# Attention scores of both maps in one PSUM tile of five banks, with one maximum and one exponential per map

## The chip, the cores and the metric

The kernel runs on one core of a Trainium2 chip. A core has five engines, each with its own queue that runs in order: TensorE (PE) multiplies matrices and writes PSUM; VectorE (DVE), ScalarE (ACT) and GpSimd (POOL) work element by element; SyncE (SP) issues transfers. PSUM is 16 KB per partition, eight banks of 512 fp32 numbers. Engines wait for each other through semaphores that the program sets. The metric is the time in microseconds of one whole execution on the device.

## The reference, cut to what matters

The program is one step of a network with two layers, for a prompt of 256 tokens and a sample of 1024. The change lies in the differential attention of layer 0: per head two score maps, two softmaxes, and the difference of the two applied to the values. The sample sees 256 cached keys as well as its own 1024.

```python
def _diff_attn(q, k, v, lam):          # 8 heads (H_B), 2 maps, DH = 64
    ...
    def block(qi):                     # 128 queries
        s = jnp.einsum('bqhmd,bkhmd->bhmqk', qi.astype(F32), kf) * (DH ** -0.5)
        p = jax.nn.softmax(s, axis=-1)
        a = p[:, :, 0] - lam * p[:, :, 1]
        return jnp.einsum('bhqk,bkhe->bqhe', a, vf)
    ...
# sample: k = 256 cached keys and 1024 own ones; prompt: its own 256
```

## The kernel before, in words

The attention is `stage_b`. Its unit is a tile of 128 queries of one head. A head has ten: tiles 0 to 7 (`qt < 8`) are the sample's, with 1280 keys, and tiles 8 and 9 the prompt's, with 256. Eight heads follow each other, 80 tiles in all. The loop at the end of `stage_b` is written as a software pipeline, and the order in it is the order on the engines PE, DVE, ACT and POOL (`tc.manual_schedule`). In the round of tile t:

- PE: `scores(t)`, twelve matmuls (per map 1024 sequence keys in two halves of 512 and 256 cached keys, each once with the queries' high part `qh` and once with the low part `ql`); in tiles 8 and 9 a step of the next head's value projection (`PRE`); two transposes of the tile before last (`turn(p, 8)`); every second tile the value product of a pair (`values`, 30 matmuls, `pv`); steps of a projection that fills gaps (`FILL`, 24 matmuls a step, `acc`); eight transposes of the last tile (`turn(u, 0)`, `turn(u, 4)`).
- DVE: `maxima(t, 0)`, `maxima(t, 1)`, `ratio(t)`, `combine(t, 0)`, then the low parts `atl` of the transposes.
- ACT: `exps(t, 0)`, `exps(t, 1)`, then casts of weights (`whi`) and of transposes (`ath`), copies, and the scaling in `combine(t, 1)`, whose sum POOL makes.

The scores lie in three PSUM tiles: X0 and X1 (two banks each, 1024 sequence keys of map 0 and 1) and Y (one bank, the cached keys of both maps side by side; in tiles 8 and 9 the prompt's keys). Two more PSUM pools hold the transposes (`pt`, two buffers of one bank) and the products (`pa`, one bank). So a map has two maxima, joined by a minimum of their negatives (L1007), two exponentials, and two sums, joined in `ratio` (L1020). X0 and X1 also serve as PSUM for the value transposes `vt` of the next head (ten in tile 9, L948) and X1 for a small product `mp` (16 matmuls at the end of tile 9, read by DVE at L85; in the last head in tile 8).

A PSUM tile is the unit by which the framework keeps order: what writes or reads it waits for the other engines' earlier work on the same tile.

```python
seq(0)                                               # X0
for m in range(2):
    dot(t.Y[:, m], m, hd.kx[m][:, LS:] if t.qt < 8 else hd.kp[m])
seq(1)                                               # X1
```

Of the kernel before, what the change touches and what calls it, by code (L numbers as in the profile page):

```python
# [904 lines left out]
def stage_b(c, wp):  # L905
# [5 lines left out]
    with ExitStack() as es:  # L911
# [18 lines left out]
        def value_steps(h):  # L930
# [12 lines left out]
            for i in range(0, 10, n):  # L943
                w = min(n, 10 - i)
                p = (ps.tile([128, 8, 128], F32, name="vt", tag=f"X{i // 8}") if h else
# [32 lines left out]
        def scores(t):  # L978

            t.X, t.Y = [None] * 2, ps.tile([128, 2, 256], F32, name="Y")  # L980
            q, hd = t.q, t.hd
            t.mx = sm.tile([128, 2, 2], F32, name="mx")
            t.sums = sm.tile([128, 2, 2], F32, name="sums")
            t.e = [wk.tile([128, 1280], F32, name=f"e{m}", bufs=3 - m) for m in range(2)]

            def dot(out, m, keys):
# [3 lines left out]
            def seq(m):  # L990
                if t.qt < 8:
                    t.X[m] = ps.tile([128, 1024], F32, name=f"X{m}", tag=f"X{m}")
                    for k in (0, 512):
                        dot(t.X[m][:, k:k + 512], m, hd.kx[m][:, k:k + 512])
            seq(0)
            for m in range(2):
                dot(t.Y[:, m], m, hd.kx[m][:, LS:] if t.qt < 8 else hd.kp[m])
            seq(1)

        def maxima(t, m):  # L1000
            b = t.mx[:, 1, m:m + 1]
# [1005 lines left out]
```

## Time and profile before

| | |
|---|---|
| median of 3 runs | 2843.38 us (2842.13 to 2846.84) |
| the profiled execution | 2840.99 us, of it 2839.2 us span |
| PE, DVE, ACT, POOL busy in the span | 91%, 64%, 38%, 23% |
| `stage_b`, from the first score | 788 to about 1500 us |
| one head in it (heads 2 to 7) | about 88 us |

A row of a timeline gives start, length, engine, line and operation with output<-input, and in brackets how long the engine had stood idle and what ended it. A matmul's end is modelled: the next starts some 0.23 us after it (512 columns) although its row is 0.39 us long. Rows of equal instructions are merged (x10).

### The profile page before, as it was taken

The page shows a single profiled execution, that of the slowest core. Times are in us where ns is not written, and L with a number is a line of the kernel's source. Part 1 is how long each engine was busy: PE and PEld are TensorE (multiplying, and loading weights), DVE is VectorE, ACT ScalarE, POOL GpSimd, SP SyncE. Part 2 cuts the span into 40 slices and gives each one's busy share as a digit, 9 for nine tenths or more (in the row PEclk, how much of TensorE's full clock was granted, in tenths as well). Part 3 has the DMA queues.
Part 4 walks back from the last instruction along what each step waited for, and adds up shares of the span by engine and source line. Part 5 has one row for each costly group of instructions (what it writes and reads, how often), then busy time and mean ns, then how long its engine had stood idle before and what let it go on. Part 6 is the DMA issues. An engine that isn't in the chain of part 4 may idle for free.

```text
span 2839.2 us, 40047 instructions
## 1 busy us (share of the span) xinstructions
PE 2587.4 (91%) x14905; PEld 2254.6 (79%) x14905; DVE 1826.1 (64%) x3570; ACT 1072.1 (38%) x2136; POOL 660.4 (23%) x508
## 2 busy tenths in 40 slices
PE   8999889986689999999988789988999999999998
PEld 6777777765578888888876667767999989999786
DVE  6889999997367778777777962575234435654332
ACT  3342233211156667666663221463223333322311
POOL 0000000000023223232234443316223324432321
PEclk9999999987899999999999899998999999999999
DMA  5534566466722222122216772322322136654422
GB/s 221 179 113 116 168 205 199 160 200 164 186 73 81 86 81 80 54 90 86 75 58 192 240 246 84 108 86 80 109 78 74 61 98 225 202 169 152 148 79 93
DMA packets 232490, 368.76 MB, mean 130 GB/s; under 512 B 31044, under 2 KB 155494, under 8 KB 228710
## 3 DMA queue, kind: packets, MB, share of 16 engines
q1 hardware_dynamic: 200520, 315.03, 34.9%
q10 hardware_dynamic: 31632, 50.53, 6.0%
q8 instruction: 117, 1.92, 0.3%
q14 instruction: 77, 0.63, 0.1%
q0 software_dynamic: 144, 0.66, 0.1%
HBM read 248.82 MB, written 104.73 MB: 125 GB/s over the span
## 4 chain that ended last, share of the span: by engine, by line
PE 41%; DVE 14%; ACT 5%; DMA 4%; POOL 2%; issue 2%; SPq 0%; DVEq 0%; ACTq 0%; POOLq 0%
PE pf L47 6%; PE pf L46 6%; PE pf L48 6%; PE oa L48 3%; PE oa L47 3%; PE oa L46 3%; DVE mx L1003 2%; ACT e L1013 2%; DVE mrt L131 2%; DVE atl L1047 2%; PE acc L46 1%; PE acc L47 1%; PE acc L48 1%; DVE e L1031 1%; DMA owf<-w_out_o 1%
## 5 line engine op out<-in xcount | busy, mean ns | idle before, releaser
L48 PE MATMUL acc<-hhi,wlo 128*128 128x512 f32 (+1 forms) x1152 | 414.0, 361 | 32.2 <-DVE wlo L42 32.2
L46 PE MATMUL acc<-hhi,whi 128*128 128x512 f32 (+1 forms) x1152 | 417.8, 363 | 11.1 <-ACT O L1056 6.5
L47 PE MATMUL acc<-hlo,whi 128*128 128x512 f32 (+1 forms) x1152 | 414.3, 360 | 0.8 <-DVE hlo L218 0.2
L1034 POOL TENSOR_TENSOR e<-e,e 128x1024 f32<-128x1024 f32 x64 | 152.5, 2382 | 1104.1 <-DMA vh<-dVc 799.7
L48 PEld LDWEIGHTS acc<-hhi,wlo 128*128 128x128 f32 x1152 | 220.2, 191 | 70.0 <-DVE wlo L42 39.6
L48 PE MATMUL oa<-owh,oyl 128*128 128x512 f32 x640 | 254.3, 397 | 6.3 <-POOL oyl L42 6.3
L46 PEld LDWEIGHTS acc<-hhi,whi 128*128 128x128 f32 x1152 | 220.8, 192 | 46.5 <-ACT O L1056 11.0
L46 PE MATMUL oa<-owh,oyh 128*128 128x512 f32 x640 | 253.6, 396 | 2.3 <-ACT gt L1269 1.1
L47 PE MATMUL oa<-owl,oyh 128*128 128x512 f32 x640 | 252.9, 395 | 0.0
L47 PEld LDWEIGHTS acc<-hlo,whi 128*128 128x128 f32 x1152 | 220.6, 191 | 33.2 <-DVE hlo L218 3.4
L1013 ACT ACTIVATE e<-X,mx 128x1024 f32<-128x1024 f32 x128 | 142.8, 1116 | 120.7 <-DVE mx L1007 117.6
L42 POOL TENSOR_TENSOR wlo<-wf,whi 128x512 fp32r<-128x512 f32 x80 | 111.2, 1389 | 297.0 <-ACT whi L41 277.9
L41 ACT CAST whi<-wf 128x512 fp32r<-128x512 f32 x146 | 89.7, 620 | 211.1 <-DMA wf<-w_glu 43.7
L1003 DVE TENSOR_REDUCE mx<-X 128x1 f32<-128x1024 f32 x128 | 155.2, 1212 | 18.0 <-PE X L988 18.0
L42 DVE TENSOR_TENSOR wlo<-fold,whi 128x512 fp32r<-128x512 f32 x94 | 85.4, 922 | 108.0 <-ACT whi L41 107.0
L48 PEld LDWEIGHTS oa<-owh,oyl 128*128 128x128 f32 x640 | 120.8, 189 | 37.6 <-POOL oyl L42 9.9
L46 PEld LDWEIGHTS oa<-owh,oyh 128*128 128x128 f32 x640 | 120.7, 189 | 32.4 <-DVE t L1366 2.1
L1366 DVE TENSOR_TENSOR t<-oa,gate 128x512 f32<-128x512 f32 x60 | 41.3, 690 | 160.2 <-PE oa L48 157.2
L47 PEld LDWEIGHTS oa<-owl,oyh 128*128 128x128 f32 x640 | 120.7, 189 | 27.9
L1046 ACT CAST ath<-atp 128x512 fp32r<-128x512 f32 (+1 forms) x208 | 99.3, 513 | 103.2 <-PE atp L1043 101.8
L46 PE MATMUL pf<-heh,whi 128*128 128x322 f32 x400 | 126.0, 319 | 9.9 <-ACT heh L1527 8.2
L1047 DVE TENSOR_TENSOR atl<-atp,ath 128x512 fp32r<-128x512 f32 (+1 forms) x208 | 115.2, 579 | 18.5 <-ACT ath L1046 18.5
(450 smaller groups left out, 6969.9 us busy)
## 6 DMA issues: line engine op xcount, KB each, us to landing
wf<-w_in_e SPq DMA_DIRECT2D x96, 256.0 KB
raw<-w_fno SPq DMA_DIRECT2D x16, 1024.0 KB
mw<-w_mod SPq DMA_DIRECT2D x24, 512.0 KB
stg<-w_modT SPq DMA_DIRECT2D x24, 512.0 KB
u<-dU SPq DMA_DIRECT2D x16, 640.0 KB
dz<-z SPq DMA_DIRECT2D x8, 1280.0 KB
zc<-dz SPq DMA_DIRECT2D x16, 640.0 KB
qh<-dQh SPq DMA_DIRECT2D x160, 64.0 KB
```

Of the source, the lines that this page charges most:

```text
L41: nc.scalar.copy(hi, src)
L42: (le or nc.gpsimd).tensor_sub(lo, src, hi.bitcast(F32))
L46: nc.tensor.matmul(out, whi, xhi, start=start, stop=False)
L47: nc.tensor.matmul(out, whi, xlo, start=False, stop=False)
L48: nc.tensor.matmul(out, wlo, xhi, start=False, stop=stop)
L131: nc.vector.scalar_tensor_tensor(t, w, 0.5, s.cond[:, g], op0=OP.mult, op1=OP.mult, accum_out=acc[:, g:g + 1])
L1003: v.tensor_reduce(t.mx[:, 0, m:m + 1], t.X[m], axis=AX.X, op=OP.max, negate=True)
L1013: nc.scalar.activation(t.e[m][:, :LS], t.X[m], AF.Exp, bias=b, accum_out=t.sums[:, 0, m:m + 1])
L1034: nc.gpsimd.tensor_add(e[0][:, nk:], e[0][:, nk:], e[1][:, nk:])
L1046: nc.scalar.copy(hi, p[:, :w])
L1047: return lambda: v.tensor_sub(t.al[:, b:b + w, o], p[:, :w], hi.bitcast(F32))
L1366: nc.vector.tensor_mul(t, acc[j, m], gate(j // 8)[:, o])
```

## The change

One tile S of five banks, 2560 numbers per partition, takes the place of X0, Y and X1 for the whole stage. Map 0 has columns 0 to 1279 and map 1 columns 1280 to 2559, so that the third bank holds the end of map 0 and the start of map 1. The twelve matmuls stay, in the order map 0 first half, map 0 second half, map 1's first 256 keys, map 0's cached keys, then the rest of map 1. One maximum and one exponential over 1280 columns serve a map; the sum goes straight to where `ratio` reads it, and the minimum (L1007) and the addition (L1020) fall away. Tiles 8 and 9 use columns 1024 to 1535. `vt` takes columns 0 to 1023 and from 1536 on, `mp` columns 1536 to 1663.

```diff
+        S = ps.tile([128, 2560], F32, name="S")
...
-                p = (ps.tile([128, 8, 128], F32, name="vt", tag=f"X{i // 8}") if h else
+                p = (S[:, (0, FIRST1)[i // 8]:][:, :w * 128].rearrange("p (a b) -> p a b", b=128) if h else
...
-            seq(0)
-            for m in range(2):
-                dot(t.Y[:, m], m, hd.kx[m][:, LS:] if t.qt < 8 else hd.kp[m])
-            seq(1)
+            if t.qt < 8:
+                for m, k0, k1 in ((0, 0, 512), (0, 512, 1024), (1, 0, 256), (0, 1024, 1280), (1, 256, 768), (1, 768, 1280)):
+                    dot(m * 1280 + k0, m, hd.kx[m][:, k0:k1])
...
-                v.tensor_reduce(t.mx[:, 0, m:m + 1], t.X[m], axis=AX.X, op=OP.max, negate=True)
-            if m == 0:
-                v.tensor_reduce(t.mx[:, 1], t.Y, axis=AX.X, op=OP.max, negate=True)
-            if t.qt < 8:
-                v.tensor_tensor(b, t.mx[:, 0, m:m + 1], b, op=OP.min)
+                v.tensor_reduce(t.mx[:, m:m + 1], S[:, m * 1280:m * 1280 + 1280], axis=AX.X, op=OP.max, negate=True)
...
-                nc.scalar.activation(t.e[m][:, :LS], t.X[m], AF.Exp, bias=b, accum_out=t.sums[:, 0, m:m + 1])
-            nc.scalar.activation(t.e[m][:, y0:y0 + 256], t.Y[:, m], AF.Exp, bias=b, accum_out=t.sums[:, 1, m:m + 1])
+            nc.scalar.activation(t.e[m][:, :n], S[:, o:o + n], AF.Exp, bias=t.mx[:, m:m + 1], accum_out=t.hd.s[:, m, t.qt:t.qt + 1])
...
-            if t.qt < 8:
-                v.tensor_add(sc, t.sums[:, 0], t.sums[:, 1])
...
-                    c.mod[0].product(*mw, ps.tile([2, 128], F32, name="mp", tag="X1"))
+                    c.mod[0].product(*mw, S[:2, FIRST1:FIRST1 + 128])
...
+FIRST1 = 1536
```

What stands on the engines now is shown at three places; in brackets is the engine whose semaphore an instruction waits for (Activation_49 is ACT's, DMAHW a transfer's).

DVE, from the ratio of tile 3 of a head to the second maximum of tile 4, before:

```order
L1020 TENSOR_TENSOR s<-sums 128x2 [waits Activation_49]
L1024 RECIPROCAL r<-s 128x1 [waits DVE_49]
L1025 SCALAR_TENSOR_TENSOR r<-r,s,nlam 128x1 [waits DVE_49]
L1031 SCALAR_TENSOR_TENSOR e_11764<-e_11765,r,e_11764 128x256 [waits DVE_49,Pool_49]
L1047 TENSOR_TENSOR atl<-atp,ath 128x4x128 [waits Activation_49] x2
L1003 TENSOR_REDUCE mx<-X_11861 128x1 [waits PE_49]
L1005 TENSOR_REDUCE mx<-Y 128x2 [waits PE_49]
L1007 TENSOR_TENSOR mx<-mx 128x1 [waits DVE_49]
L1047 TENSOR_TENSOR atl<-atp,ath 128x2x128 [waits Activation_49]
L1003 TENSOR_REDUCE mx<-X_11870 128x1
L1007 TENSOR_TENSOR mx<-mx 128x1 [waits DVE_49]
```

and the same stretch after:

```order
L1013 RECIPROCAL r<-s 128x1 [waits Activation_49]
L1014 SCALAR_TENSOR_TENSOR r<-r,s,nlam 128x1 [waits DVE_49]
L1020 SCALAR_TENSOR_TENSOR e_11288<-e_11289,r,e_11288 128x256 [waits DVE_49,Pool_49]
L1036 TENSOR_TENSOR atl<-atp,ath 128x4x128 [waits Activation_49] x2
L1000 TENSOR_REDUCE mx<-S 128x1 [waits PE_49]
L1036 TENSOR_TENSOR atl<-atp,ath 128x2x128 [waits Activation_49]
L1000 TENSOR_REDUCE mx<-S 128x1 [waits Activation_49]
```

Eleven instructions have become eight (a row with x2 is two). The second maximum, which waited for nothing, now waits for ACT: in the built program the value is that of the first exponential of its own tile. The first maximum's wait for PE has moved from map 0's fourth matmul to the twelfth of the tile.

PE, the scores of tile 3 of a head (the two `kx` names are the keys of map 0 and of map 1), before:

```order
L987 MATMUL X_9846<-kx_9379,qh 128x512 [waits DMAHW7_49,DMAHW0_49,Activation_49]
L988 MATMUL X_9846<-kx_9379,ql 128x512 [waits DMAHW2_49,DMAHW1_49]
L987 MATMUL X_9846<-kx_9379,qh 128x512
L988 MATMUL X_9846<-kx_9379,ql 128x512
L987 MATMUL Y<-kx_9379,qh 128x256 [waits Activation_49]
L988 MATMUL Y<-kx_9379,ql 128x256
L987 MATMUL Y<-kx_9380,qh 128x256
L988 MATMUL Y<-kx_9380,ql 128x256
L987 MATMUL X_9855<-kx_9380,qh 128x512
L988 MATMUL X_9855<-kx_9380,ql 128x512
```

and after:

```order
L988 MATMUL S<-kx_9122,qh 128x512 [waits DMAHW7_49,DMAHW0_49,Activation_49]
L989 MATMUL S<-kx_9122,ql 128x512 [waits DMAHW2_49,DMAHW1_49]
L988 MATMUL S<-kx_9122,qh 128x512
L989 MATMUL S<-kx_9122,ql 128x512
L988 MATMUL S<-kx_9123,qh 128x256
L989 MATMUL S<-kx_9123,ql 128x256
L988 MATMUL S<-kx_9122,qh 128x256
L989 MATMUL S<-kx_9122,ql 128x256
L988 MATMUL S<-kx_9123,qh 128x512
L989 MATMUL S<-kx_9123,ql 128x512
```

Before, the first wait for ACT was for the exponential that frees X0 and the second, at Y, for the last exponential of the tile ahead. Now there is one, at the first matmul, and it is for the last exponential of the tile ahead.

PE in tile 9, where the ten value transposes follow the prompt's scores (`kp` are its keys), before:

```order
L987 MATMUL Y<-kp_8617,qh 128x256
L988 MATMUL Y<-kp_8617,ql 128x256
L948 MATMUL vt<-ident,x 128x128 x8
L948 MATMUL vt<-ident,x 128x128 [waits Activation_49]
L948 MATMUL vt<-ident,x 128x128
L1043 MATMUL atp<-ident,e_9280 128x128 [waits DVE_49]
```

and after:

```order
L988 MATMUL S<-kp_8440,qh 128x256
L989 MATMUL S<-kp_8440,ql 128x256
L950 MATMUL S<-ident,x 128x128 [waits DVE_49]
L950 MATMUL S<-ident,x 128x128 x7
L950 MATMUL S<-ident,x 128x128 [waits DVE_49]
L950 MATMUL S<-ident,x 128x128
L1032 MATMUL atp<-ident,e_9031 128x128 [waits PE_49]
```

The first transpose now waits for the maximum of tile 9 on DVE, and the ninth for DVE's `vl`, the difference that reads the first eight.

## Rows read from the trace of the kernel before

**Rows 1.** The attention: length, busy us of PE, PEld, DVE, ACT, POOL; clock.

```profile
788.00:1500.00 712.00, 665.95 (x4090) 573.81 (x4088) 523.09 (x1041) 448.42 (x991) 215.28 (x113) 0.97 0.26 77
```

**Rows 2.** Groups by line and shape there: busy us, mean ns | idle before.

```profile
L1003 DVE TENSOR_REDUCE mx<-X 128x1 f32<-128x1024 f32 x128 | 155.2, 1212 | 18.0 <-PE X L988 18.0
...
L1013 ACT ACTIVATE e<-X,mx 128x1024 f32<-128x1024 f32 x128 | 142.8, 1116 | 120.7 <-DVE mx L1007 117.6 <-DVE zb L1084 0.4
...
L1014 ACT ACTIVATE e<-Y,mx 128x256 f32<-128x256 f32 x160 | 74.8, 471 | 0.0
...
L1005 DVE TENSOR_REDUCE mx<-Y 128x2 f32<-128x512 f32 x80 | 54.3, 679 | 0.0
...
L1007 DVE TENSOR_TENSOR mx<-mx 128x1 f32<-128x1 f32 x128 | 47.0, 367 | 4.4
...
L1020 DVE TENSOR_TENSOR s<-sums 128x2 f32<-128x2 f32 x64 | 10.4, 162 | 84.1 <-ACT e L1014 84.1
...
L950 DVE TENSOR_TENSOR vl<-vt,vh 128x1024 fp32r<-128x1024 f32 x7 | 8.6, 1225 | 1.0 <-ACT vh L949 0.3
...
L949 ACT CAST vh<-vt 128x1024 fp32r<-128x1024 f32 x7 | 7.1, 1015 | 3.0 <-PE vt L948 3.0
```

**Rows 3.** Timeline of PE in the sixth head: where tiles begin, and tile 9.

```profile
1235.47 0.48 PE L987 MATMUL X<-kx,qh 128*128 128x512 f32 x1
...
1268.49 0.48 PE L987 MATMUL X<-kx,qh 128*128 128x512 f32 x1
...
1270.66 0.40 PE L988 MATMUL X<-kx,ql 128*128 128x512 f32 x1
...
1277.55 0.48 PE L987 MATMUL X<-kx,qh 128*128 128x512 f32 x1
...
1303.65 0.39 PE L987 MATMUL Y<-kp,qh 128*128 128x256 f32 x1 [0.76 <-ACT e L1014]
...
1309.59 0.36 PE L987 MATMUL Y<-kp,qh 128*128 128x256 f32 x1
...
1310.15 1.25 PE L948 MATMUL vt<-ident,x 128*128 128x128 f32 x10
1311.23 0.38 PE L1043 MATMUL atp<-ident,e 128*128 128x128 f32 x2
...
1323.37 0.48 PE L987 MATMUL X<-kx,qh 128*128 128x512 f32 x1
```

**Rows 4.** Timeline of ACT in the same head, around exponentials.

```profile
1267.47 1.11 ACT L1013 ACTIVATE e<-X,mx 128x1024 f32<-128x1024 f32 x1
1268.48 0.19 ACT L1013 ACTIVATION_READ_ACCUMULATOR e<-X,mx 128x1 f32 x1
...
1303.40 0.20 ACT L1014 ACTIVATION_READ_ACCUMULATOR e<-Y,mx 128x1 f32 x1
```

**Rows 5.** Timeline of DVE in the same head.

```profile
1267.21 0.16 DVE L1007 TENSOR_TENSOR mx<-mx 128x1 f32<-128x1 f32 x1
...
1311.48 0.68 DVE L1005 TENSOR_REDUCE mx<-Y 128x2 f32<-128x512 f32 x1
...
1323.28 0.28 DVE L85 TENSOR_TENSOR mwb<-mp,mwb 2x128 f32<-2x128 f32 x1 [8.01 <-PE mp L84]
```

**Rows 6.** PE by stretch: length, busy us, granted clock (1.00 is 2.4 GHz).

```profile
62.30:64.30 2.00, 0.00 (x0) 1.00 0.00 0
64.30:68.30 4.00, 3.97 (x17) 0.57 0.00 0
862.00:864.00 2.00, 0.69 (x5) 1.00 0.88 315
864.00:868.00 4.00, 3.70 (x30) 1.00 0.27 72
1253.00:1255.00 2.00, 0.99 (x5) 1.00 0.32 104
1256.00:1262.00 6.00, 6.00 (x26) 0.50 0.13 37
```

More of the change, by code (lines that the diff above doesn't have):

```diff
@@ L978, in scores, with dot @@
         def scores(t):
-            t.X, t.Y = [None] * 2, ps.tile([128, 2, 256], F32, name="Y")
             q, hd = t.q, t.hd
-            t.mx = sm.tile([128, 2, 2], F32, name="mx")
-            t.sums = sm.tile([128, 2, 2], F32, name="sums")
+            t.mx = sm.tile([128, 2], F32, name="mx")
             t.e = [wk.tile([128, 1280], F32, name=f"e{m}", bufs=3 - m) for m in range(2)]
-            def dot(out, m, keys):
+            def dot(o, m, keys):
+                out = S[:, o:o + keys.shape[1]]
@@ L987, in dot @@
                 nc.tensor.matmul(out, q[0][:, m], keys, start=True, stop=False)
                 nc.tensor.matmul(out, q[1][:, m], keys, start=False, stop=True)
-            def seq(m):
-                if t.qt < 8:
-                    t.X[m] = ps.tile([128, 1024], F32, name=f"X{m}", tag=f"X{m}")
-                    for k in (0, 512):
-                        dot(t.X[m][:, k:k + 512], m, hd.kx[m][:, k:k + 512])
-            seq(0)
-            for m in range(2):
-                dot(t.Y[:, m], m, hd.kx[m][:, LS:] if t.qt < 8 else hd.kp[m])
@@ L998, in scores @@
-            seq(1)
+            if t.qt < 8:
+                for m, k0, k1 in ((0, 0, 512), (0, 512, 1024), (1, 0, 256), (0, 1024, 1280), (1, 256, 768), (1, 768, 1280)):
+                    dot(m * 1280 + k0, m, hd.kx[m][:, k0:k1])
+            else:
+                for m in range(2):
+                    dot(1024 + m * 256, m, hd.kp[m])
         def maxima(t, m):
-            b = t.mx[:, 1, m:m + 1]
             if t.qt < 8:
-                v.tensor_reduce(t.mx[:, 0, m:m + 1], t.X[m], axis=AX.X, op=OP.max, negate=True)
@@ L1004, in maxima @@
-            if m == 0:
-                v.tensor_reduce(t.mx[:, 1], t.Y, axis=AX.X, op=OP.max, negate=True)
-            if t.qt < 8:
-                v.tensor_tensor(b, t.mx[:, 0, m:m + 1], b, op=OP.min)
-        def exps(t, m):
-            y0 = LS if t.qt < 8 else 0
-            b = t.mx[:, 1, m:m + 1]
-            if t.qt < 8:
-                nc.scalar.activation(t.e[m][:, :LS], t.X[m], AF.Exp, bias=b, accum_out=t.sums[:, 0, m:m + 1])
-            nc.scalar.activation(t.e[m][:, y0:y0 + 256], t.Y[:, m], AF.Exp, bias=b, accum_out=t.sums[:, 1, m:m + 1])
+                v.tensor_reduce(t.mx[:, m:m + 1], S[:, m * 1280:m * 1280 + 1280], axis=AX.X, op=OP.max, negate=True)
+            elif m == 0:
+                v.tensor_reduce(t.mx, S[:, 1024:1536].rearrange("p (m k) -> p m k", m=2), axis=AX.X, op=OP.max, negate=True)
@@ L1016, in ratio @@
+        def exps(t, m):
+            n = 1280 if t.qt < 8 else 256
+            o = m * 1280 if t.qt < 8 else 1024 + m * 256
+            nc.scalar.activation(t.e[m][:, :n], S[:, o:o + n], AF.Exp, bias=t.mx[:, m:m + 1], accum_out=t.hd.s[:, m, t.qt:t.qt + 1])
         def ratio(t):
             sc = t.hd.s[:, :, t.qt]
-            if t.qt < 8:
-                v.tensor_add(sc, t.sums[:, 0], t.sums[:, 1])
-            else:
-                v.tensor_copy(sc, t.sums[:, 1])
             t.r = sm.tile([128, 1], F32, name="r")
```

## The prediction, made before the changed kernel ran

> **What bounds the kernel now.** The page's busy shares come first, then the attention alone, since only it changes. From 788 to 1500 us PE is busy 666 of 712 us at a granted clock of 0.97 [rows 1]; DVE and ACT have a fifth to a third of the time free. So PE sets the time there, and all that shorter work on DVE and ACT could ever win is the 46 us in which PE stands idle. Next come the starts of tiles on PE in the sixth head, whose pattern the heads around it repeat: tile 0 begins at 1235.47, tile 8 at 1303.65, tile 9 at 1309.59, the next head at 1323.37 [rows 3]. That is 68.2 us for the eight sample tiles, 5.9 for tile 8, 13.8 for tile 9. Eight tiles in 68.2 us are 8.5 us each; a chain through DVE and ACT that is longer than this, and that PE has to wait for, shows at once.
>
> **What falls away.** Per tile DVE loses one minimum after each maximum and one addition, and the maxima of 1024 and of 512 become two of 1280. From 679 ns for 512 columns and 1212 for 1024 [rows 2] a column costs 1.04 ns; a maximum over 1280 comes to 1.48 us. The exponentials cost 471 and 1116 ns for 256 and 1024 [rows 2], so 0.84 ns a column, 1.33 us for 1280. With the read of the accumulator a 1024 exponential lasts from 1267.47 to 1268.67, 1.20 us [rows 4]; one of 1280 then 1.42, against 1.20 and about 0.46 for the two. Per tile ACT saves some 0.4 us, and DVE 0.25 on maxima and 0.5 on small instructions (L1007 at a mean of 367 ns, L1020 at 162 [rows 2]).
>
> **What is added: waits.** The order on the engines, with what each instruction waits for, shows three.
>
> First, the scores of a tile no longer start when X0 is free but when the last exponential of the tile ahead is done. Second, the first maximum waits for all twelve matmuls, not for four. Third, the second maximum waits for the first exponential. Before, the second maximum ran beside the first exponential and the next tile's scores beside the second. Now scores, maximum, exponential, maximum, exponential stand in one line, and the next scores follow the last.
>
> The length of that line, from the start of the scores: twelve matmuls 2.57 us (1268.49 to the end of the twelfth at 1271.06 [rows 3]); hand-off to DVE 0.05 (an estimate from the one below); maximum 1.48; hand-off to ACT 0.10 (L1007 ends 1267.37 [rows 5], the exponential starts 1267.47 [rows 4]); exponential 1.42; hand-off to DVE 0.03 to 0.05, taken as 0.03; maximum 1.48; hand-off 0.10; exponential 1.42; hand-off to PE 0.05 (1303.60 [rows 4] to 1303.65 [rows 3]). Sum 8.70 us. DVE's other work after the exponential (reciprocal, ratio, `combine`, two `atl`, about 2.2 us with the casts they wait for) lies beside the next scores and stays hidden; behind the waiting maximum stand only `atl` and steps of `finish`, which fit in the exponentials.
>
> A tile now takes 8.70 us or PE's own work, whichever is longer. PE's work is longer only in tiles 4 and 6, with a whole projection step of 24 matmuls of 512 columns: 9.06 in tile 4 (1268.49 to 1277.55 [rows 3]), and about 9.4 in tile 6, which adds four transposes of `finish`. So the eight tiles take 6 x 8.70 + 9.06 + 9.4 = 70.7 us against 68.2: **2.5 us more per head**. The saving of 0.4 us on ACT and 0.75 on DVE is already in this.
>
> **Tile 9** pays more. In it PE runs the ten transposes `vt` at 1310.15, right after the scores [rows 3]. In the same tile S the first must wait for DVE's maximum, which starts at 1311.48 and lasts 0.68 [rows 5], because DVE is still at the `atl` of tile 7. So PE stands still until 1312.21. Eight transposes take 1.03 (ten take 1.25 [rows 3]); then the ninth waits for ACT's cast, 1.02, and DVE's `vl`, 1.23 [rows 2], with hand-offs of 0.13 in all; the last two take 0.22. They end at 1315.84 instead of 1311.23: 4.6 us, all of it on PE, since `values`, a projection step and `mp` are queued behind and nothing in tile 9 waits for another engine for as long. At the end the next head's first scores wait for L85, which ends 1323.56 [rows 5], instead of starting at 1323.37 [rows 3]: 0.24. Together **4.85 us in each of seven heads**; the last head has no `vt`. There `mp` waits in tile 8 for that tile's exponentials, about 1.3 us, and one of its tiles is already over 13 us long through a transfer of weights, so that this one loses nothing: 2.8 us in all. Tile 8 keeps its 5.9 us: its exponentials and the POOL sum before its transposes count from the last exponential of tile 7, as before.
>
> Sum without the clock: 7 x (2.5 + 4.85) + 2.8 = 54 us.
>
> **The clock** has no one price. After 2.0 idle us PE worked at 0.57 for the next 4 us; after 1.3 idle us in a stretch of 2 it stayed at 1.00; in the sixth head two short waits (1253 to 1255) followed by one-column products led to 6 us at 0.50, that is 1.2 GHz [rows 6]. Such a slow stretch stands in tiles 2 and 3 of every head already, where PE has slack. Now PE idles some 3 us at the end of tile 2 (twenty one-column matmuls are most of its work), and the scores of tile 3, which lie in the line, run at half speed: 0 to 2.3 us, taken as 1.7, in eight heads. In tile 9 PE idles 2.06 and then 2.3 us with one busy us between; a slow stretch of 4 to 8 us after that costs 2 to 4, but partly falls into the idle time: 0 to 4, taken as 1.8, in seven heads. In the other tiles PE idles 0.7 to 1.7 us, nearer to the 1.3 us row without a drop: nothing. Sum 26 us; ends 0 and 46.
>
> 54 + 26 = 80 us on the profiled execution's 2841 is 2921, and the median lies 2.4 above that execution. I take **2922 us**.
>
> **Rivals.**
>
> *The waits cost nothing* and the savings reach PE. For it: DVE and ACT are what PE's idle time waits for, and 1.15 us per tile go. The Trainium skill speaks for it ("Perfetto Trace Analysis", section Optimizing Scalar/DVE Operations): grouping into larger operations improves throughput where the engine is saturated. The rows agree that an instruction has a fixed part (0.15 us in a maximum), but no engine but PE is saturated here. Against it: the waits stand in the program. It would hold if the next scores could start early in banks already read. PE's 46 idle us [rows 1] are the ceiling; the part that waits for DVE and ACT, about 4.5 us a head, gives 2841 - 36 + 2 = 2807. The Trainium skill ("PSUM — Partial Sum Buffer", section PSUM bank collisions raise a hardware error) says only that two engines must not touch one bank at once, reads included. By that rule alone the second maximum must wait, for the shared third bank, but the next scores could begin in the first two banks; the sum would be near this rival's 2807. The waits at the first score and at the first maximum, though, go by the whole tile.
>
> *The line is shorter than laid out.* If the accumulator's read lies outside it (0.1 each) and maxima hand over before their rows end (about 0.1 each), the line is 8.3 us: six tiles give back 0.4 each, 2.4 a head, 19 in all. With the clock at its lower end: 2843 + 54 - 19 = 2878. For it: instructions that follow each other on one engine start before the one ahead has ended. Against: other engines start after the row's end wherever the rows show it.
>
> *PE loses its clock in every waiting tile.* Idle times of 0.7 to 1.7 us in tiles 0, 1, 5 and 7 also bring half speed, and twelve matmuls at half speed add up to 2.3 us to the line: 4 x 2.3 x 8 = 74, so about 2995. Against it: the 1.3 us row.
>
> **How the numbers follow.** Forecast, the line and `vt` on PE's path with some loss of clock: 0.72, alone 2893 to 2950. The shorter line: 0.12, at 2878. Clock lost everywhere: 0.10, at 2995. Waits free: 0.04, at 2807; the two effects cancel within 0.2%, which is what a measurement of this kernel tells from no change: 0.02. The range must leave out at most 0.2: 2878 less a margin for its hand-offs, 2874, up to 2955 leaves out the free waits, the cancelling and the lost clock, 0.16, and some tail. Faster 0.04, same 0.02, slower 0.94.
>
> **What would show it.** Right: in the profile after, the second maximum's idle time is ended by the first exponential and PE's first score by the second; six of eight tiles take 8.5 to 8.9 us from score to score; `vt` splits into eight and two with about 2.3 us between; DVE's and ACT's busy time fall although the span grows. Wrong: tiles below 8.4 us mean a shorter line; scores that start under the exponentials mean that the waits are not those I read; slow stretches outside tiles 2, 3 and 9 mean the clock. A slowdown outside 788 to 1500 us would be something that I have not seen.

## The result, and the profile after

The changed kernel takes 2930.14 us in the median (2926.36 to 2931.66) against 2842.76 for the kernel before, a ratio of 1.0303 (95% interval 1.0286 to 1.0321). The forecast was 2922 us in a range of 2874 to 2955. The profiled execution of after has a span of 2929.9 us, 90.7 more than that of before.

First the attention as a whole: length, busy time of PE, PEld, DVE, ACT and POOL, granted clock, to be held against [rows 1].

```profile
791.00:1585.00 794.00, 687.96 (x4065) 591.12 (x4064) 457.91 (x765) 419.78 (x729) 217.04 (x112) 0.93 0.23 68
```

DVE and ACT are busy for less time than before, 458 against 523 us and 420 against 448, and the stretch is still 82 us longer. What was saved on two engines did not reach the end. PE's idle time grew from 46 to 106 us, and its busy time, for the same matmuls, from 666 to 688, at a granted clock of 0.93 instead of 0.97.

The groups there that answer to [rows 2] (busy us, mean ns | idle before, and what ended it):

```profile
L1000 DVE TENSOR_REDUCE mx<-S 128x1 f32<-128x1280 f32 x128 | 190.9, 1491 | 148.2 <-ACT e L1007 82.0 <-PE S L989 65.9
L1007 ACT ACTIVATE e<-S,mx 128x1280 f32<-128x1280 f32 x128 | 170.1, 1329 | 177.3 <-DVE mx L1000 152.8 <-DVE var L1058 11.3 <-DVE rs_ia L56 11.3
L988 PE MATMUL S<-kx,qh 128*128 128x512 f32 x256 | 115.7, 452 | 41.4 <-ACT e L1007 41.3
...
L950 PE MATMUL S<-ident,x 128*128 128x128 f32 x70 | 12.5, 314 | 28.9 <-DVE vl L952 16.5 <-DVE mx L1002 12.3
```

The wide maximum costs 1.49 us and the wide exponential 1.33, as laid out (1.48, 1.33). The right-hand side is the news: DVE's maximum waits for an exponential (82 us), the exponential for a maximum (153 us), and PE's scores for an exponential (41 us). Before, PE's 512-column scores waited for next to nothing:

```profile
L987 PE MATMUL X<-kx,qh 128*128 128x512 f32 x256 | 111.6, 436 | 0.3 <-ACT e L1013 0.3
```

One tile of the sixth head, to be read downwards as the line it is (start, length, engine, line, and in brackets how long the engine stood idle and what ended it):

```profile
1296.58 0.50 PE L988 MATMUL S<-kx,qh 128*128 128x512 f32 x1
...
1299.21 1.49 DVE L1000 TENSOR_REDUCE mx<-S 128x1 f32<-128x1280 f32 x1 [1.00 <-PE S L989]
...
1300.74 1.33 ACT L1007 ACTIVATE e<-S,mx 128x1280 f32<-128x1280 f32 x1 [3.25 <-DVE mx L1000]
...
1302.19 1.49 DVE L1000 TENSOR_REDUCE mx<-S 128x1 f32<-128x1280 f32 x1 [1.49 <-ACT e L1007]
...
1303.72 1.33 ACT L1007 ACTIVATE e<-S,mx 128x1280 f32<-128x1280 f32 x1 [1.56 <-DVE mx L1000]
1304.94 0.19 ACT L1007 ACTIVATION_READ_ACCUMULATOR e<-S,mx 128x1 f32 x1
...
1305.19 0.50 PE L988 MATMUL S<-kx,qh 128*128 128x512 f32 x1 [0.32 <-ACT e L1007]
```

2.63 us to the first maximum, 1.53 to the first exponential, 1.45 to the second maximum, 1.53 to the second exponential, 1.47 to the next scores: 8.61 us. While one of the three engines works on the scores, the other two have nothing to do with them.

The lengths of the ten tiles of the sixth head, from PE's first score to the next tile's first score, in us. Kernels that are told of below stand beside them:

| tile | 0 | 1 | 2 | 3 | 4 | 5 | 6 | 7 | 8 | 9 | head |
|---|---|---|---|---|---|---|---|---|---|---|---|
| before | 7.99 | 7.51 | 9.61 | 7.91 | 9.06 | 7.71 | 9.92 | 8.47 | 5.94 | 13.78 | 87.90 |
| after | 8.61 | 8.60 | 8.67 | 10.70 | 8.94 | 8.65 | 9.37 | 8.64 | 5.94 | 20.78 | 98.90 |
| e1 old instructions on S | 9.59 | 9.84 | 11.16 | 10.95 | 9.73 | 9.94 | 9.72 | 10.46 | 6.70 | 21.12 | 109.21 |
| e3 `vt` later | 8.60 | 8.61 | 8.68 | 10.71 | 8.93 | 8.66 | 9.38 | 8.65 | 5.93 | 14.07 | 92.22 |
| e5 maxima first | 8.39 | 8.34 | 8.35 | 10.38 | 8.95 | 8.33 | 9.36 | 8.30 | 5.95 | 21.99 | 98.34 |
| e9 filler in `ms` | 8.59 | 8.61 | 8.68 | 8.66 | 8.94 | 8.65 | 9.37 | 8.66 | 5.94 | 20.02 | 96.12 |
| e2 two tiles | 7.99 | 7.51 | 7.47 | 9.02 | 8.88 | 7.47 | 9.34 | 7.24 | 5.69 | 14.00 | 84.61 |
| e6 two tiles, old instructions | 7.99 | 7.51 | 8.44 | 9.61 | 8.92 | 7.71 | 9.94 | 7.46 | 6.96 | 14.22 | 88.76 |
| e11 three banks a map | 8.00 | 9.18 | 9.11 | 10.10 | 10.54 | 10.26 | 12.08 | 10.03 | 7.25 | 14.01 | 100.56 |

In after, five of the tiles that the forecast put on the line stand at 8.60 to 8.67, whatever PE has to do in them. Tile 3 and tile 9 stand out. Tile 9, in the same head:

```profile
1374.70 0.37 PE L988 MATMUL S<-kp,qh 128*128 128x256 f32 x1
...
1376.38 0.68 DVE L1002 TENSOR_REDUCE mx<-S 128x2 f32<-128x512 f32 x1
1377.12 1.10 PE L950 MATMUL S<-ident,x 128*128 128x128 f32 x8 [1.71 <-DVE mx L1002]
1378.25 1.01 ACT L951 CAST vh<-S 128x1024 fp32r<-128x1024 f32 x1 [2.36 <-PE S L950]
1379.30 1.23 DVE L952 TENSOR_TENSOR vl<-S,vh 128x1024 fp32r<-128x1024 f32 x1 [2.23 <-ACT vh L951]
1380.58 0.69 PE L950 MATMUL S<-ident,x 128*128 128x128 f32 x2 [2.36 <-DVE vl L952]
1381.06 0.63 PE L1032 MATMUL atp<-ident,e 128*128 128x128 f32 x2
...
1395.15 0.28 DVE L85 TENSOR_TENSOR mwb<-S,mwb 2x128 f32<-2x128 f32 x1 [10.92 <-PE S L84]
1395.48 0.50 PE L988 MATMUL S<-kx,qh 128*128 128x512 f32 x1
```

The ten value transposes, one block of 1.25 us in [rows 3], are eight and two with 2.36 idle us between and 1.71 ahead. They end 6.36 us after the tile's first score, against 1.64 before.

The clock, by stretches of PE (length, busy us of PE, ..., granted clock in the third figure from the end):

```profile
1318.70:1319.90 1.20, 1.20 (x10) 0.81 (x9) 0.50 (x1) 0.67 (x2) 0.28 (x1) 1.00 0.36 106
1319.90:1322.46 2.56, 0.01 (x2) 0.00 (x1) 1.43 (x5) 1.47 (x3) 0.00 (x0) 0.67 0.09 26
1322.46:1327.20 4.74, 4.74 (x15) 3.86 (x15) 2.20 (x6) 2.48 (x4) 3.72 (x2) 0.50 0.16 59
1378.20:1380.50 2.30, 0.02 (x1) 0.00 (x0) 1.20 (x1) 1.01 (x1) 0.00 (x0) 0.63 0.34 97
1380.50:1385.60 5.10, 5.02 (x24) 5.02 (x25) 1.74 (x6) 1.77 (x6) 0.00 (x0) 0.50 0.00 0
```

The first three stretches are the end of tile 2 and the scores of tile 3, the last two lie in tile 9. In both places PE stands idle for over two us with the clock falling, and then works at 0.50, which is 1.2 GHz: all twelve scores of tile 3, and two thirds of the value product in tile 9.

### The profile page after: what moved, and what is told of

Its sections match the earlier page's. It is cut to its first block, busy times and chain, and to the rows that moved or that the text cites. A ratio compares the mean times of both kernels' runs of the same rounds, so it can differ in the third digit from the quotient of the medians.

```text
span 2929.9 us, 39494 instructions
## 1 busy us (share of the span) xinstructions
PE 2616.3 (89%) x14905; PEld 2280.8 (78%) x14905; DVE 1760.9 (60%) x3298; ACT 1045.3 (36%) x1880; POOL 665.8 (23%) x508
## 4 chain that ended last, share of the span: by engine, by line
PE 47%; DVE 15%; ACT 7%; DMA 5%; issue 2%; POOL 1%; ACTq 0%; SPq 0%; DVEq 0%; POOLq 0%
PE pf L47 6%; PE pf L46 6%; PE pf L48 6%; DVE mx L1000 6%; ACT e L1007 5%; PE oa L48 4%; PE oa L47 4%; PE oa L46 4%; PE S L988 3%; PE S L989 3%; DVE mrt L131 2%; PE acc L46 1%; PE acc L47 1%; PE acc L48 1%; DMA m<-kt 1%
## 5 line engine op out<-in xcount | busy, mean ns | idle before, releaser
L1000 DVE TENSOR_REDUCE mx<-S 128x1 f32<-128x1280 f32 x128 | 190.9, 1491 | 148.2 <-ACT e L1007 82.0
L1007 ACT ACTIVATE e<-S,mx 128x1280 f32<-128x1280 f32 (+1 forms) x160 | 185.0, 1158 | 178.4 <-DVE mx L1000 152.8
L42 POOL TENSOR_TENSOR wlo<-wf,whi 128x512 fp32r<-128x512 f32 x80 | 117.8, 1472 | 314.7 <-ACT whi L41 270.4
L988 PE MATMUL S<-kx,qh 128*128 128x512 f32 (+1 forms) x384 | 148.9, 401 | 41.4 <-ACT e L1007 41.3
L989 PE MATMUL S<-kx,ql 128*128 128x512 f32 (+1 forms) x384 | 142.2, 383 | 0.0
```

Source lines behind the costliest of these rows:

```text
L42: (le or nc.gpsimd).tensor_sub(lo, src, hi.bitcast(F32))
L1000: v.tensor_reduce(t.mx[:, m:m + 1], S[:, m * 1280:m * 1280 + 1280], axis=AX.X, op=OP.max, negate=True)
L1007: nc.scalar.activation(t.e[m][:, :n], S[:, o:o + n], AF.Exp, bias=t.mx[:, m:m + 1], accum_out=t.hd.s[:, m, t.qt:t.qt + 1])
```

## The experiments

The theory after the result was the one of the forecast: one PSUM tile puts scores, maxima and exponentials of a tile in one line, tile 9 pays for the place of `vt`, and the clock falls in the gaps. The rivals: that the wide instructions cost, that the shared bank costs, or that the line is set by something else. All edits are against the changed kernel unless something else is said.

**e1: the waits without the merge.** One tile S, with the instructions of the kernel before on it:

```diff
-                v.tensor_reduce(t.mx[:, m:m + 1], S[:, m * 1280:m * 1280 + 1280], axis=AX.X, op=OP.max, negate=True)
+                v.tensor_reduce(t.mx[:, 0, m:m + 1], S[:, m * 1536:m * 1536 + 1024], axis=AX.X, op=OP.max, negate=True)
+            if m == 0:
+                v.tensor_reduce(t.mx[:, 1], S[:, 1024:1536].rearrange("p (m k) -> p m k", m=2), axis=AX.X, op=OP.max, negate=True)
+            if t.qt < 8:
+                v.tensor_tensor(b, t.mx[:, 0, m:m + 1], b, op=OP.min)
...
+                nc.scalar.activation(t.e[m][:, :LS], S[:, m * 1536:m * 1536 + 1024], AF.Exp, bias=b, accum_out=t.sums[:, 0, m:m + 1])
+            nc.scalar.activation(t.e[m][:, y0:y0 + 256], S[:, 1024 + m * 256:1280 + m * 256], AF.Exp, bias=b, accum_out=t.sums[:, 1, m:m + 1])
```

> One PSUM tile S for both maps as in the changed kernel, but the separate maxima, minima, exponentials and sums of the kernel before on it, so that only the waits are new. Theory (the waits on the whole tile make the loss, the wide instructions give a part of it back): scores 2.6, two maxima and a minimum 2.0, hand-off 0.1, two exponentials 1.66, second maximum and minimum 1.4, 0.1, two exponentials 1.66, 0.1 stand in one line, 9.6 us, longer than PE's work in every sample tile; about 7 us more per head than the changed kernel, so about 2985 (2960 to 3010). Rival (the wide instructions over 1280 columns are what costs): the time falls back to about 2843.

Measured: 3012.53 us (3010.89 to 3014.17), ratio 1.0582 (1.0561 to 1.0603). The second maximum waits for the exponentials here too:

```profile
1352.23 1.22 DVE L1002 TENSOR_REDUCE mx<-S 128x1 f32<-128x1024 f32 x1 [1.00 <-PE S L990]
...
1356.04 1.23 DVE L1002 TENSOR_REDUCE mx<-S 128x1 f32<-128x1024 f32 x1 [1.79 <-ACT e L1013]
```

The tiles without loss of clock came out as laid out, 9.6 to 9.9 us. The total is 27 us above the forecast and just outside its range, since tiles 2 and 3 of the heads take about 11 us (in the sixth at granted clocks of 0.68 and 0.86); tile 7, 10.5 us at full clock, was not followed up. That the wide instructions cost is excluded: with the narrow ones the same waits are some 80 us dearer (1.0582 against 1.0303).

**e2: the merge without the waits.** S is cut at a bank into two PSUM tiles. The first holds map 0 and map 1's cached keys, so that one maximum and one exponential still do for map 0; map 1 keeps two of each. The cached keys of map 1 are exponentiated first, so that the first tile comes free early. Eight value transposes go to the second tile and two to the transposes' pool.

```diff
-        S = ps.tile([128, 2560], F32, name="S")
+        S0 = ps.tile([128, 1536], F32, name="S0")
+        S1 = ps.tile([128, 1024], F32, name="S1")
...
+                if m == 0:
+                    mx(t.mx[:, 0:1], S0[:, 0:1280])
+                    mx(t.mx[:, 2:3], S0[:, 1280:1536])
+                else:
+                    mx(t.mx[:, 3:4], S1)
+                    v.tensor_tensor(t.mx[:, 1:2], t.mx[:, 2:3], t.mx[:, 3:4], op=OP.min)
...
+            elif m == 0:
+                a(t.e[m], S0[:, 0:1280], sc)
+            else:
+                a(t.e[m][:, LS:], S0[:, 1280:1536], t.sums[:, 1:2])
+                a(t.e[m][:, :LS], S1, t.sums[:, 0:1])
```

> Two PSUM tiles, cut at a bank: the first (three banks) holds map 0's 1280 columns and map 1's 256 cached keys, the second (two banks) map 1's 1024. One maximum and one exponential for map 0, two of each for map 1; eight of the value transposes in the second tile, two in the transposes' pool, the small product in the second tile. Theory (the order by whole tile costs, the wide instructions do not): the line falls apart again, tiles return to about 7.5 to 9.9 us as PE's work has it, and what DVE and ACT save takes up to 1 us a head from PE's waits: 2836 (2828 to 2846). Rival (a maximum or exponential over columns of three banks, or the shared third bank, costs): 2880 or more.

Measured: 2816.4 us (2810.91 to 2817.91), ratio **0.9889** (0.9875 to 0.9904). It is faster than both kernels, and below the range that was expected. The end of tile 2 in the fifth head, in order of time:

```profile
1156.00 1.33 ACT L1013 ACTIVATE e<-S,mx 128x1280 f32<-128x1280 f32 x1 [1.72 <-DVE mx L1001]
1156.22 1.21 DVE L1001 TENSOR_REDUCE mx<-S 128x1 f32<-128x1024 f32 x1
...
1158.18 1.11 ACT L1013 ACTIVATE e<-S,mx 128x1024 f32<-128x1024 f32 x1
1158.33 0.56 PE L990 MATMUL S<-kx,qh 128*128 128x512 f32 x1 [0.72 <-ACT e L1013]
```

The second maximum (from 1156.22) runs beside the first exponential (from 1156.00), and PE writes the next scores (from 1158.33) while ACT still reads the other tile (1158.18 to 1159.29). That is the overlap that one tile takes away. For the next scores it is the whole tile that matters in after, since they begin in banks that map 1's exponential does not read; whether the shared third bank alone would hold back the second maximum, no run separates. The rule cited in the forecast, of the Trainium skill ("PSUM — Partial Sum Buffer", section PSUM bank collisions raise a hardware error), forbids only two engines on one bank; this trace agrees with it, at a cut that lies between banks. The shared third bank is still there, in the first tile, and costs nothing that shows.

**e6: the two tiles without the merge.** e2 with the separate maxima, minima, exponentials and sums of the kernel before.

```diff
-                    mx(t.mx[:, 0:1], S0[:, 0:1280])
-                    mx(t.mx[:, 2:3], S0[:, 1280:1536])
...
+                mx(t.mx[:, 0, m:m + 1], S1 if m else S0[:, 0:1024])
+            if m == 0:
+                mx(t.mx[:, 1], S0[:, 1024:1536].rearrange("p (m k) -> p m k", m=2))
...
+            y = lambda: a(t.e[m][:, y0:y0 + 256], S0[:, 1024 + m * 256:1280 + m * 256], t.sums[:, 1, m:m + 1])
+            x = lambda: a(t.e[m][:, :LS], S1 if m else S0[:, 0:1024], t.sums[:, 0, m:m + 1])
+            for f in ((x, y), (y, x))[m] if t.qt < 8 else (y,):
+                f()
```

> The two tiles of the run that was faster (three banks with map 0 and the cached keys of both, two banks with map 1's 1024), the same places for the value transposes and the small product and the same order of map 1's exponentials, but with the separate maxima, minimum, exponentials and sums of the kernel before. Theory (that run's 31 us come from map 0's merged maximum and exponential, some 0.4 us of DVE and 0.25 of ACT a tile): the gain is gone, 2845 (2836 to 2858). Rival (they come from the other cut of the tiles, by which the next scores no longer wait for the last exponential): it stays, 2812 to 2825.

Measured: 2846.23 us (2842.03 to 2853.65), ratio 1.0006 (0.9995 to 1.0018). So the other cut gives nothing by itself, and e2's whole gain is that of the merge. One head of each, the sixth of e6 and then the fifth of e2 (length, busy PE, PEld, DVE, ACT, POOL; the granted clock is the third figure from the end):

```profile
1242.20:1330.96 88.76, 83.51 (x515) 72.00 (x515) 66.02 (x133) 55.73 (x123) 26.65 (x14) 0.96 0.25 78
```

```profile
1135.60:1220.05 84.45, 81.17 (x517) 71.24 (x515) 61.36 (x123) 53.93 (x107) 26.68 (x14) 0.98 0.28 82
```

DVE loses 4.7 us a head, ACT 1.8, and the head becomes 4.3 shorter, although DVE was busy only 66 of 89 us. PE's side of it: 2.0 us less idle time (5.25 against 3.28), and 2.3 us less busy time for the same matmuls (83.5 against 81.2), at a granted clock of 0.98 instead of 0.96. Over the second to the seventh head the means are 2.2 and 2.0 us. So the gain is not idle time alone: up to half of it is PE's own work, done faster. How much of that the head's length hangs on is not separated. In the table the gain lies mostly in tiles 2, 3, 6 and 8. The Trainium skill ("Perfetto Trace Analysis", section Optimizing Scalar/DVE Operations) says that larger operations help where an engine is saturated, and that where it isn't but leaves bubbles on others, breaking instructions up may let work finish sooner. Here the fewer, larger instructions paid on an engine that is not saturated: what PE waits for became shorter. In after the bubbles come from the one tile and not from the size of the instructions: broken up on the same tile, in e1, they made the kernel slower still.

**e3: `vt` elsewhere on PE.** Still one tile S; the eight transposes stand behind the value product of tile 9, the two behind the next projection step.

```diff
                     if p.qt < 9:
                         values(p)
+                        if qt == 9 and hd.h + 1 < HB:
+                            steps(fill, 1)
...
+                vts = fill.pop(0) if qt == 9 and t and hd.h + 1 < HB else None
+                if vts:
+                    steps(fill, 1)
+                    list(vts)
-PRE = {8: 1, 9: 1}
+PRE = {8: 1}
```

> The changed kernel with the ten value transposes of tile 9 moved on TensorE's queue behind the value product (eight) and behind one projection step after it (two), where what they wait for is done. Theory (5 us of waits and some 2 us of lost clock in tile 9 are those of the transposes' place): tile 9 falls from 20.7 to about 14.5 us in seven heads, 44 us in all, 2886 (2880 to 2895). Rival (tile 9 is long through something else, such as the next head's scores waiting for L85 or DVE's work): 2915 or more.

Measured: 2881.1 us (2875.57 to 2882.77), ratio 1.0117 (1.0102 to 1.0132).

```profile
1340.20 1.03 PE L950 MATMUL S<-ident,x 128*128 128x128 f32 x8
...
1343.83 0.38 PE L950 MATMUL S<-ident,x 128*128 128x128 f32 x2
```

No wait stands ahead of either, and tile 9 falls from 20.78 to 14.07 us: 6.7 us in each of seven heads, 47 of the 49 us gained. The price of tile 9 is the place of `vt` in a tile that DVE still reads.

**e5: both maxima first.**

```diff
                 if t:
                     maxima(t, 0)
+                    maxima(t, 1)
...
-                    maxima(t, 1)
                     exps(t, 1)
```

> The changed kernel with the second maximum queued on DVE right behind the first, ahead of the first exponential. Theory (scores, maxima and exponentials stand in one line in any case, so their order costs nothing and back to back they save hand-offs): 8.61 us become about 8.36 in the five or six tiles of a head that the line sets, 10 to 12 us in all, 2919 (2914 to 2926). Rival (the second maximum was hidden beside other work and the line is set by something else): no gain, or up to 1.45 us more in each tile, 2930 to 3000.

Measured: 2907.69 us (2906.68 to 2908.05), ratio 1.0212 (1.0195 to 1.0230).

```profile
1291.96 2.89 DVE L1000 TENSOR_REDUCE mx<-S 128x1 f32<-128x1280 f32 x2 [0.72 <-PE S L989]
```

```profile
1294.89 1.33 ACT L1007 ACTIVATE e<-S,mx 128x1280 f32<-128x1280 f32 x1 [1.84 <-DVE mx L1000]
...
1296.21 1.32 ACT L1007 ACTIVATE e<-S,mx 128x1280 f32<-128x1280 f32 x1
```

The first exponential now begins a whole maximum later, and the tile is shorter: 8.33 us instead of 8.61 to 8.65. So nothing runs beside the second maximum in after; the line is what sets the tile. In the second to the last head this brings 1.7 us each, as expected; the gain is twice the expected one, and outside its range, because another 8 us come from the first head, whose tiles are longer in after than those of the others (below).

**e8: e3 and e5 together**, with the edits of both and nothing else.

> One tile S as in the changed kernel, with both edits that helped it: the value transposes later on TensorE's queue and the second maximum right behind the first. Theory (two separate prices of the one tile, so the gains of 49 and 22 us add; the line of 8.35 us and TensorE's own tiles 4 and 6 then give 90.4 us a head, still 2.4 more than the kernel before): 2862 (2854 to 2870), above the kernel before. Rival (with those two places mended the merged instructions pay, as they do in two tiles): 2843 or less.

Measured: 2862.81 us (2860.89 to 2867.36), ratio 1.0066 (1.0050 to 1.0081); the sixth head takes 90.37 us. The two gains add, and one tile stays behind the kernel before even so. What is left is mostly not the length of the line, which is 8.31 to 8.38 us here. Of the 2.5 us by which the sixth head is longer, 2.2 lie in the sample tiles, and 0.26 in tile 9. Tile 3 alone takes 10.38 us, with PE at a granted clock of 0.50 in its first 4.8 us, and so stands 2.0 above the line; with it on the line (an estimate), the eight sample tiles would sum to 68.3 us against 68.2 before. Whether this kernel with e9's filler would reach the kernel before was not run.

**e4: the clock, first try.** Ten matmuls that nobody needs, at the end of tile 2, in a buffer of the pool of products.

```diff
+                    if qt == 2:
+                        nop = pa.tile([128, 512], F32, name="nop", tag="acc")
+                        for _ in range(10):
+                            nc.tensor.matmul(nop, t.q[0][:, 0], t.hd.kx[0][:, 0:512], start=True, stop=True)
```

> The changed kernel with ten needless matmuls of 512 columns at the end of tile 2 of every head, where TensorE stands idle for 2.55 us before the scores of tile 3; they write a PSUM buffer that nobody reads. Theory (the twelve matmuls of tile 3 run at half speed because TensorE stood idle ahead of them, and they lie in the line): with the gap filled they run at full speed, tile 3 falls from 10.7 to about 8.7 us although there is more work, 16 us in all, 2914 (2908 to 2922). Rival (tile 3 is long through DVE or ACT, the clock falls beside work that waits anyway): no change, 2928 to 2935, and the filler may add to it.

Measured: 2938.73 us (2931.99 to 2942.91), ratio 1.0329 (1.0305 to 1.0352).

```profile
1224.80 4.64 PE L1153 MATMUL nop<-kx,qh 128*128 128x512 f32 x10 [1.61 <-DVE var L1060]
```

A miss in the building: the pool has one buffer, in which `ms` stood, and the filler waits until DVE has read that. So the gap stayed, and the filler ran at half speed in the place of the scores (0.46 us a matmul). In the sixth head tile 2 grew by 3.5 us and tile 3 shrank by 1.3. It settles nothing.

**e9: the clock, second try.** The filler in `ms`'s own tile, right behind the one-column products, where it waits for nothing new.

```diff
-            ms = pa.tile([128, 10], F32, name="ms", tag="acc")
+            ms = pa.tile([128, 512], F32, name="ms", tag="acc")
+            nop, ms = ms[:, 128:512], ms[:, 0:10]
...
+                for _ in range(13):
+                    nc.tensor.matmul(nop, w.q[0][:, 0], w.hd.kx[0][:, 0:384], start=True, stop=True)
```

> The changed kernel with thirteen needless matmuls of 384 columns (2.2 us) right behind the twenty one-column matmuls of tile 2, in seven heads, into the same PSUM tile, so that they wait for nothing that those did not wait for; the eight transposes then end shortly before the scores of tile 3 may start. Theory (the 2.55 us that TensorE stands idle there bring the half speed in which the scores of tile 3 run): without the idle time the clock stays, tile 3 falls from 10.7 to 8.7 us in seven heads, 14 us in all, 2916 (2911 to 2922). Rival (the one-column matmuls ahead bring it, or it falls whatever is done there): tile 3 keeps its length, 2926 to 2940.

Measured: 2912.47 us (2906.64 to 2915.77), ratio 1.0241 (1.0216 to 1.0265). PE around the start of tile 3, and then the clock there:

```profile
1309.79 2.54 PE L1061 MATMUL ms<-kx,qh 128*128 128x384 f32 x13
1312.17 1.03 PE L1032 MATMUL atp<-ident,e 128*128 128x128 f32 x8
1313.57 0.51 PE L988 MATMUL S<-kx,qh 128*128 128x512 f32 x1 [0.37 <-ACT e L1007]
```

```profile
1313.60:1316.40 2.80, 2.80 (x16) 2.41 (x17) 2.31 (x6) 2.45 (x4) 1.82 (x2) 1.00 0.16 47
```

More work, and less time: with the idle time down from 2.55 to 0.37 us the clock stays at 1.00, and tile 3 falls from 10.70 to 8.66 us, in the seven heads that have the filler alike. The 2.0 us of tile 3 are the clock's. The run also shows the clock in tile 9: with the same waits there, that tile takes 20.0 to 20.1 us in three heads, at a mean granted clock of 0.91 or 0.92, and 21.8 to 22.1 in three others, at 0.77; in after it is 20.6 to 21.0, at 0.83 or 0.84.

**e10: the same in the two-tile kernel**, with four such matmuls.

```diff
+                for _ in range(4):
+                    nc.tensor.matmul(nop, w.q[0][:, 0], w.hd.kx[0][:, 0:384], start=True, stop=True)
```

> The two-tile kernel that was faster than the kernel before, with four such needless matmuls (0.7 us) behind the one-column ones. Theory (in it TensorE waits 0.7 us at the end of tile 2 and works at half speed in tile 3, 8.5 to 9.8 us instead of about 7.3): tile 3 becomes 1.2 us shorter in seven heads, 2808 (2802 to 2815). Rival (so short an idle time is not what brings the half speed there): 2814 to 2822.

Measured: 2810.57 us (2809.0 to 2812.02), ratio 0.9884 (0.9863 to 0.9905), which is e2's within the interval; it was run on another occasion than e2, so that only the ratios compare.

```profile
1234.81 2.96 PE L1073 MATMUL ms<-ones,sq 128*128 128x1 f32 x20 [0.42 <-DVE zb L901]
1237.64 1.63 PE L1077 MATMUL ms<-kx,qh 128*128 128x384 f32 x4
```

In this, the sixth head, the slow stretch begins among the one-column products already (2.96 us against 2.39 at full clock), and the filler itself runs in it. The fourth head tells more, since there the clock stays at 1.00 through tiles 2 and 3:

```profile
1064.94 2.39 PE L1073 MATMUL ms<-ones,sq 128*128 128x1 f32 x20 [0.40 <-DVE zb L901]
...
1068.99 0.50 PE L990 MATMUL S<-kx,qh 128*128 128x512 f32 x1
...
1072.84 0.44 PE L1048 MATMUL atp<-ident,e 128*128 128x128 f32 x2 [1.26 <-DVE atl L1052]
```

And yet tile 3 takes 8.51 us, as in e2's fourth head, where it ran at 0.83 (8.50). At full clock PE waits 1.26 us for DVE in it instead. So in this kernel the half speed of such a head costs nothing. Tiles 2 and 3 together take 15.8 us in heads 2 to 4 of e10 and 17.2 to 17.3 in heads 5 to 8, where the slow stretch is longer; in e2 15.8 in four of these heads and 16.5 to 17.1 in the three others. That filling the gap gains what it did in after does not hold here.

**e7: real work for the gap.** The two-tile kernel with the short projection step in tile 2 instead of tile 1.

```diff
-FILL = (2, 1, 0, 0, 2, 0, 2, 0, 0, 2)
+FILL = (2, 0, 1, 0, 2, 0, 2, 0, 0, 2)
```

> The two-tile kernel with the short projection step (24 matmuls of 256 columns) moved from tile 1 to tile 2 of each head. Theory (in it, too, TensorE waits 0.7 us at the end of tile 2 and then works at half speed in tile 3, for about 1.3 us a head; the step fills that gap, and tile 1 falls to the 6.2 us of the shorter line): 10 us less from the clock, 4 more from tile 1, 2810 (2804 to 2816). Rival (tile 1 cannot get shorter than 6.6 us, since the value product's transposes wait there for POOL, or the clock falls elsewhere): 2816 to 2830.

Measured: 2837.63 us (2832.16 to 2844.92), ratio 0.9977 (0.9967 to 0.9988).

```profile
1167.98 0.58 PE L46 MATMUL acc<-hhi,whi 128*128 128x256 f32 x1 [1.87 <-DVE var L1076]
```

Tile 1 fell to 5.92 us, as laid out, but tile 2 rose to 13.4 to 14.9. It is e4's miss again: the step's buffer is the one of `ms`, PE waits 1.87 us for DVE and then runs at half speed.

**e11: three banks for each map.** One maximum and one exponential for each map, without a shared tile; the sixth bank is taken from the transposes.

```diff
-        ps, pt, pa = pool("aps", 1, space=PSUM), pool("apt", 2, space=PSUM), pool("apa", 1, space=PSUM)
+        ps, pt, pa = pool("aps", 1, space=PSUM), pool("apt", 1, space=PSUM), pool("apa", 1, space=PSUM)
...
-        S = ps.tile([128, 2560], F32, name="S")
+        SS = [ps.tile([128, 1536], F32, name=f"S{m}") for m in range(2)]
```

> One maximum and one exponential for each map as in the changed kernel, but each map in a tile of its own of three banks, so that no bank is shared; the bank for that comes from the transposes, which have one buffer instead of two. The ten value transposes stand in map 1's tile in one piece. Theory (the merge itself pays, but a second group of transposes now waits for ACT's cast and DVE's difference of the first, 1.3 us or more in each sample tile): about 1.5 us a tile more than the two-tile kernel, 2895 (2860 to 2930). Rival (the transposes' second buffer is hardly used, and without a shared bank both merges pay in full): 2816 or less.

Measured: 2956.21 us (2954.26 to 2957.55), ratio 1.0396 (1.0370 to 1.0423). PE's waits in the attention (us in total, times, longest):

```profile
PE atp L1033 <- DVE atl L1037: 113.3, 71, 4.5
PE rb L1072 <- DVE atl L1037: 19.6, 21, 1.2
...
PE S L988 <- ACT e L1008: 0.7, 1, 0.7
```

The scores wait for nothing any more (0.7 us), and the transposes for the buffer that was taken (133 us). The mechanism is the expected one, its size was put 61 us too low: 1.5 us a tile against about 2.

## Why the prediction was right, point by point

The profile's 90.7 us against the forecast's 80, by its own terms:

| term | forecast | measured |
|---|---|---|
| sample tiles of a head, without clock | +2.5 | +2.0 |
| clock, tile 3 | +1.7 | +2.0 |
| tile 9, waits of `vt` and of L85 | +4.85 | +5.0 |
| tile 9, clock | +1.8 | +2.0 |
| one head (mean of the second to the seventh) | +10.85 | +10.9 |
| first head | +10.85 | +14.65 |
| last head | +4.5 | +5.0 |
| outside the attention's tiles | 0 | +5.6 |

The sample tiles are those of the sixth head in the table, with tile 3 at e9's 8.66: 70.1 against 68.2. Tile 9: the last transpose ends 4.72 us later against its tile's start, L85 adds some 0.2 as laid out, and the rest of the 7.0 us is the half speed.

**The line** was put at 8.70 and is 8.60 to 8.67. In the tile laid out above, the 0.09 us are mainly the two hand-offs from DVE to ACT: a maximum's row ends 0.04 us before the exponential's starts, where 0.10 was taken. The tiles on it and those on PE's own work were told apart rightly: tiles 4 and 6, put at 9.06 and 9.4, took 8.94 and 9.37. e5 shows that it is one line, e1 that its length follows what stands in it, e2 that it is gone with the one tile.

**Tile 9** is confirmed in place and size, by the rows and by e3.

**The clock** was the loosest term, 26 us between 0 and 46. For tile 3 it is shown by e9. For tile 9 it is read from the rows (0.50 for 5.1 us after 2.3 idle us) and from e3, where it goes together with the waits; e9's heads show that the clock moves this tile by 2 us with the waits the same. That both terms came out near the values taken is in part luck: the rows of before left 0 to 2.3 us open for tile 3 and 0 to 4 for tile 9. The tiles of the sixth head that were given nothing for it lost nothing: they stand at 8.60 to 8.67, and the rival of 2995 falls.

**The rivals.** The shorter line (8.3 us, 2878) falls. That the waits cost nothing falls for this kernel; its 2807, the worth of the savings without the waits, is near to what e2 reaches with only map 0 merged, 2816, but not for its reason: it counted PE's idle time alone, and up to half of what the merge gains there is PE's busy time.

**Slips on which the forecast does not hang.** The ceiling of 46 us for all that DVE and ACT could ever win left out that PE's busy time can fall too (e6 and e2). The savings on DVE don't follow from the rows named: the maxima give 2 x 1.212 + 0.679 - 2 x 1.48 = 0.14 us a tile, not 0.25, and the small instructions at their means 0.90, not 0.5; together 1.04, and the measured fall of 65 us over 64 tiles is 1.02. The line uses neither. With 80 us on 2841 and 2.4 more, the sum is 2923.4, not 2922. And the stretch of DVE shown ahead of the prediction has twelve instructions before, not eleven.

**What was missed.** The first head lost 3.8 us more than the others. There ACT issues the last transfers of the stage ahead and loads its table before its first exponential, in both kernels (start of the exponential 7.1 us after the first score before, 7.0 after); before, the next scores did not have to wait for the second exponential, and now they do:

```profile
797.48 1.28 ACT L1007 ACT_TABLE_LOAD   x1 [5.00 <-DMA dG<-gt]
798.78 1.33 ACT L1007 ACTIVATE e<-S,mx 128x1280 f32<-128x1280 f32 x1
...
803.23 0.80 PE L988 MATMUL S<-kx,qh 128*128 128x512 f32 x1 [3.43 <-ACT e L1007]
```

Tile 0 of this head takes 11.49 us against 8.35, which is 2.5 more than the same tile loses in the other heads. Another 1.1 us stand in its tile 8 (7.01 against 5.94), where PE works at a granted clock of 0.67 for 5.2 us after 1.57 idle ones; in e3 the same idle time ahead of the same tile left the clock at 1.00, and why it differs is open. The forecast read its line in the sixth head and did not look for a head in which one member of it starts late. The 5.6 us outside the tiles were not followed up. 3.0 of them lie before the first score, in code that is the same, and the first score of the kernels run here begins anywhere from 785.8 to 796.1 us.

## What to carry to other kernels

A merged PSUM buffer is priced by what it orders, not by the instructions that it saves: write down, for each engine, which access it now waits for, add up the line from the first write to the next first write, and hold it against the bound engine's work tile by tile. Merge up to a cut at which the next writer can still start, here a bank boundary between two tiles; that made the same idea, for one of the two maps, worth 1.1% instead of costing 3.0%. What is moved into a gap has to be looked at for its buffer as well: twice here (e4, e7) PE stood idle again, because DVE had yet to read the buffer.

## What the runs showed that was not expected

Savings on engines that are far from full were worth more than PE's visible waits suggested: 4.7 us of DVE and 1.8 of ACT a head shortened the head by 4.3 us (e2 against e6), while the waits of PE for DVE and ACT that the trace names in the sixth head of before sum to some 3 us (the 0.76 of [rows 3] is about the longest). The rows of e6 and e2 go some way to explain it: only about half of the gain is idle time of PE, the rest is a shorter busy time at a higher granted clock.

In the sixth head of e10 the clock fell while PE ran its twenty one-column products and the filler without a break, after a wait of 0.42 us ahead of them, and was 0.61 in the 3.4 us that follow. In the fourth head of the same kernel the same products and filler, after a wait of 0.40 us, ran at 1.00, and so did the products in after. What tells the cases apart was not tried.

```profile
1240.60:1244.00 3.40, 3.40 (x13) 2.89 (x12) 3.12 (x4) 1.93 (x3) 2.44 (x2) 0.61 0.34 115
```
